# A batched matrix product bound by its transfers: the order of loads and stores in the software queue, from x w s w s to x s s w w

## The chip, the cores and the metric

The kernel runs on one core of a Trainium2 chip. Times are device microseconds of that core. A "span" is the profiled execution alone; it is about 2 us shorter than the time of the run. For each kernel that ran there is one trace, of one of its runs. The experiments ran beside runs of the kernel before on the same chip.

## The reference, cut

```
batch, m, k, n = 32, 512, 1024, 768          # float32
def reference(x, weight):
    return np.matmul(x, weight).astype(np.float32)
```

Per batch: 2.10 MB of x, 3.15 MB of weights in, 1.57 MB out. In all 167.8 MB read and 50.3 MB written.

## The kernel before

Weights and x are cast to bf16 on their way in; they go through the software queue that GpSimd (POOL) issues, and so do most stores. x comes for two batches at once. PE transposes x with an identity matrix, multiplies, and VectorE and ScalarE copy the sums to the output tile. The parts that matter:

```python
    AHEAD = 3
    LATE = 4
    HELD = 3
    # ... (cut)
    w_pool = ctx.enter_context(tc.tile_pool(name="w", bufs=4))
    x_pool = ctx.enter_context(tc.tile_pool(name="x", bufs=3))
    out_pool = ctx.enter_context(tc.tile_pool(name="out", bufs=7))
    # ... (cut)
        for b in range(B):
            if b % 2 and b + AHEAD + 1 < B:
                if b + AHEAD + 1 == B - 1:
                    load_last()
                else:
                    load_pair(b + AHEAD + 1)
            if b + AHEAD < B:
                load_w(b + AHEAD)
            if b <= B - LATE:
                if b > 0:
                    pending.append(b - 1)
                if b + AHEAD < B - HELD or b == B - LATE:
                    for at in pending:
                        nc.gpsimd.dma_start(out=out_view[at], in_=outs[at])
                    pending = []
            # ... (the last stores go to the SyncE queue; transposes, matmuls, copies)
```

With x for a pair of batches, w for the weights of one batch and s for a store of one batch, the queue repeats x w s w s. The last seven stores are held back until all loads are issued.

## Time and profile before

| | before |
|---|---|
| median of the first 3 runs | 517.4 us (517.32 to 517.96) |
| profiled run, its span | 515.96 us, 514.2 us |
| PE busy | 85% |
| the two DMA queues, share of 16 engines | 96.5% + 4.1% |
| HBM traffic over the span | 424 GB/s |

Read the strip of 40 slices first: the transfers are the resource that is never free. Then the waits: past the start, PE idles for weights (28.8 us in all) and for little else (10.2 us in short waits for VectorE). The lines are in the prediction below. One more view of the page of the kernel before: the chain that ended last, as shares of the span, and the table of issues with their time to landing (KB each, then us).

```profile
PE 61%; DMA 25%; DVE 6%; another core or an unknown queue 4%; issue 1%; SPq 1%; ACT 0%
...
w_sb<-in_weight_dram POOLq DMA_DIRECT2D x28, 1536.0 KB, 45.5
out_dram<-out_sb POOLq DMA_DIRECT2D x28, 1536.0 KB, 45.8
```

The chain spends 61% in PE although PE is not the bound: in a loop where a weight's load waits for PE to free a buffer and PE waits for a load issued 45 us ago, the path may run through either. The 45 us from issue to landing are the depth of the queue.

### The profile page before, as it was taken

How to read it: one execution, taken by the hardware profiler on the slowest of the kernel's cores; microseconds unless marked ns; L12 is line 12 of the kernel's file. 1: busy time of each engine (PE TensorE's matmuls, PEld its weight loads, DVE VectorE, ACT ScalarE, POOL GpSimd, SP SyncE). 2: the span in 40 equal slices, each digit the busy share in tenths (PEclk: the TensorE clock that was granted, in tenths of full speed). 3: DMA queues.
4: the chain of work that ended last, by engine and by line, in shares of the span. 5: the costliest groups of instructions: out<-in, count | busy, mean ns of one | idle time of the engine just before them, and what ended most of it. 6: DMA issues, size and time to landing. Idle time of an engine off the chain costs nothing.

```text
span 514.2 us, 5846 instructions
## 1 busy us (share of the span) xinstructions
PE 438.1 (85%) x2576; PEld 279.6 (54%) x2576; DVE 130.0 (25%) x196; ACT 76.1 (15%) x129; POOL 43.8 (9%) x87
## 2 busy tenths in 40 slices
PE   2808999999999797998979889798897979999992
PEld 1506566666666463664636546365564645666561
DVE  1205142323223141231413205032050510514121
ACT  0100111111121111111111111011111111110211
POOL 3000100101010100101001000100001001011000
PEclk9957999999999898898989989799898997999997
DMA  8999999999999999999999999999999999999997
GB/s 240 224 220 214 221 265 289 214 278 273 272 287 213 282 270 276 279 215 293 263 277 275 221 292 250 278 278 224 305 239 277 277 235 306 224 276 214 270 428 318
DMA packets 12904, 135.63 MB, mean 264 GB/s; under 512 B 1488, under 2 KB 1488, under 8 KB 3280
## 3 DMA queue, kind: packets, MB, share of 16 engines
q0 software_dynamic: 11664, 126.88, 96.5%
q1 hardware_dynamic: 1216, 8.39, 4.1%
q8 instruction: 20, 0.33, 0.2%
q14 instruction: 4, 0.03, 0.0%
HBM read 167.77 MB, written 50.33 MB: 424 GB/s over the span
## 4 chain that ended last, share of the span: by engine, by line
PE 61%; DMA 25%; DVE 6%; another core or an unknown queue 4%; issue 1%; SPq 1%; ACT 0%
PE pm L121 54%; DMA w_sb<-in_weight_dram 18%; DMA out_sb<-in_x_dram 7%; PE pt L76 6%; DVE xT L83 4%; DVE out_sb L133 2%; SPq L143 1%; PE pt L103 0%; DVE xT L91 0%; ACT out_sb L134 0%; SPq L140 0%
## 5 line engine op out<-in xcount | busy, mean ns | idle before, releaser
L121 PE MATMUL pm<-w_sb,xT 128*128 128x256 bf16 (+1 forms) x2048 | 356.5, 338 | 28.8 <-DMA w_sb<-in_weight_dram 28.8
L121 PEld LDWEIGHTS <-xT 128*128 128x128 bf16 x2048 | 206.3, 101 | 174.6 <-DMA w_sb<-in_weight_dram 32.1
L133 DVE COPY out_sb<-pm 128x512 f32<-128x512 f32 x64 | 44.2, 691 | 331.8 <-PE pm L121 314.5
L76 PE MATMUL pt<-ident,x_sb 128*128 128x128 f32 x496 | 79.8, 302 | 10.5 <-DVE xT L83 10.2
L76 PEld LDWEIGHTS pt<-ident,x_sb 128*128 128x128 f32 x496 | 69.2, 209 | 21.5 <-DVE xT L83 18.7
L83 DVE COPY xT<-pt 128x1024 bf16<-128x1024 bf16 x120 | 77.4, 687 | 11.0 <-PE pt L76 11.0
L132 ACT COPY out_sb<-pm 128x512 f32<-128x512 f32 x64 | 37.4, 585 | 283.6 <-PE pm L121 276.0
L134 ACT COPY out_sb<-pm 128x512 f32<-128x512 f32 x64 | 37.5, 585 | 144.1 <-PE pm L121 144.0
L68 POOL DMA_DIRECT2D w_sb<-in_weight_dram x37 | 19.7, 533 | 328.7 <-PE pm L121 298.9
L167 POOL DMA_DIRECT2D out_dram<-out_sb x28 | 15.0, 536 | 60.3 <-DMA w_sb<-in_weight_dram 22.7
L103 PE MATMUL pt<-ident,out_sb 128*128 128x128 f32 x8 | 1.9, 421 | 16.2 <-DMA out_sb<-in_x_dram 16.2
L103 PE MATMUL pt<-ident,x_sb 128*128 128x128 f32 x24 | 5.2, 377 | 10.4 <-DMA x_sb<-in_x_dram 10.3
L104 DVE CAST xT<-pt 128x512 bf16<-128x512 f32 x8 | 5.9, 734 | 31.4 <-PE pt L103 31.1
L58 POOL DMA_DIRECT2D x_sb<-in_x_dram x15 | 8.0, 533 | 33.4 <-DMA out_dram<-out_sb 22.6
L103 PEld LDWEIGHTS pt<-ident,out_sb 128*128 128x128 f32 x8 | 1.6, 218 | 16.5 <-issue 16.5
L103 PEld LDWEIGHTS pt<-ident,x_sb 128*128 128x128 f32 x24 | 4.1, 210 | 11.3 <-issue 10.2
L91 DVE COPY xT<-pt 128x1024 bf16<-128x1024 bf16 x4 | 2.6, 686 | 0.2 <-PE pt L76 0.2
L132 ACT ACT_TABLE_LOAD x1 | 1.3, 1283 | 0.7 <-PEq L221 0.7
L62 POOL DMA_DIRECT2D x_sb<-in_x_dram x1 | 0.5, 527 | 6.7 <-DMA w_sb<-in_weight_dram 6.7
masks.py:199 POOL TENSOR_SCALAR_AFFINE_SELECT ident<-ident 128x128 f32<-128x128 f32 x1 | 0.3, 287 | 0.1
masks.py:197 POOL MEMSET ident<- 128x128 f32 x1 | 0.2, 223 | 0.0
L221 POOL MEMSET const-float32-0.0<- 128x1 f32 x1 | 0.1, 98 | 0.2 <-issue 0.2
(3 smaller groups left out, 0.3 us busy)
## 6 DMA issues: line engine op xcount, KB each, us to landing
w_sb<-in_weight_dram POOLq DMA_DIRECT2D x28, 1536.0 KB, 45.5
out_dram<-out_sb POOLq DMA_DIRECT2D x28, 1536.0 KB, 45.8
x_sb<-in_x_dram POOLq DMA_DIRECT2D x15, 2048.0 KB, 52.1
w_sb<-in_weight_dram POOLq DMA_DIRECT2D x7, 768.0 KB, 38.3
out_dram<-out_sb SPq DMA_DIRECT2D x4, 768.0 KB
out_dram<-out_sb SPq DMA_DIRECT2D x2, 1536.0 KB
x_sb<-in_x_dram SPq DMA_DIRECT2D x1, 1536.0 KB
x_sb<-in_x_dram POOLq DMA_DIRECT2D x1, 1024.0 KB, 36.2
```

The source lines that it names most:

```text
L58: nc.gpsimd.dma_start(out=xs[b], in_=pair_view[b // 2])
L68: nc.gpsimd.dma_start(out=ws[b][:, at:at + n, :], in_=w_view[b, :, at:at + n, :])
L76: nc.tensor.transpose(pt[:, j, :], pairs[:, mo, j::JT], ident)
L83: nc.vector.tensor_copy(both[:, :, :, :, half, :].rearrange("p b j i r -> p j b i r"), words(b, mt + MT * half).rearrange("p j (b i r) -> ...
L103: nc.tensor.transpose(pt[:, i, :], rows[:, JT * h + i::KT], ident)
L104: nc.vector.tensor_copy(xT[:, 2 * h:2 * h + 2].rearrange("p j m r -> p j r m"), pt.rearrange("p (j r) m -> p j r m", r=2),)
L121: nc.tensor.matmul(pm[bank][:, at:at + size], xT[:, ko // 2, :, ko % 2], ws[b][:, ko, off:off + size], start=(ko == 0 and not (together an ...
L132: nc.scalar.copy(o[:, 0:512], pm[0])
L133: nc.vector.tensor_copy(o[:, 512:1024], pm[1])
L134: nc.scalar.copy(o[:, 1024:N2], pm[2])
L143: nc.sync.dma_start(x_fourth[rows, 0], x_view[0, rows, MT - 1])
L167: nc.gpsimd.dma_start(out=out_view[at], in_=outs[at])
```

## The change

Its intent: let loads and stores alternate less, and let no weight be followed by a store. Two stores follow each pair of x, two weights follow the stores.

```diff
+            if 0 < b <= B - LATE:
+                pending.append(b - 1)
+            if b % 2 and b + AHEAD < B - HELD:
+                flush()
             if b + AHEAD < B:
                 load_w(b + AHEAD)
-            if b <= B - LATE:
-                if b > 0:
-                    pending.append(b - 1)
-                if b + AHEAD < B - HELD or b == B - LATE:
-                    for at in pending:
-                        nc.gpsimd.dma_start(out=out_view[at], in_=outs[at])
-                    pending = []
+            if b == B - LATE:
+                flush()
```

`flush()` issues the stores in `pending` and empties it. Sizes, counts, buffers and all other engines' work stay.

More of the change, by code (lines that the diff above doesn't have):

```diff
@@ L153, with flush @@
         pending = []
+        def flush():
+            while pending:
+                at = pending.pop(0)
+                nc.gpsimd.dma_start(out=out_view[at], in_=outs[at])
         for b in range(B):
```

## The prediction

> **What bounds the kernel now.** I read the profile page from the top, then the chain of waits, then the timeline of one pair of batches, then the landings of the single transfers. The first view is the strip of 40 slices with the queues below it.
>
> ```profile
> PE   2808999999999797998979889798897979999992
> ...
> DMA  8999999999999999999999999999999999999997
> ...
> q0 software_dynamic: 11664, 126.88, 96.5%
> q1 hardware_dynamic: 1216, 8.39, 4.1%
> ...
> HBM read 167.77 MB, written 50.33 MB: 424 GB/s over the span
> ```
>
> The reader is to see that the DMA row is at 9 from the second slice to the second last, while PE shows 7s and 8s in the second half. The two queues together fill 100.6% of the 16 engines' span (above 100% because packets overlap a little). 218.1 MB in 514.2 us is 424 GB/s: the kernel is bound by its transfers, and the engines never stand without one.
>
> Second, the list of waits (who waited for whom, us in total, times, the longest):
>
> ```profile
> PE pm L121 <- DMA w_sb<-in_weight_dram: 28.8, 10, 3.8
> ...
> POOL out_dram L167 <- DMA w_sb<-in_weight_dram: 22.7, 8, 3.4
> ```
>
> and the timeline (start and length in us, then what, and in brackets PE's idle time before it) at the start of two even batches:
>
> ```profile
> 265.86 12.25 PE L121 MATMUL pm<-w_sb,xT 128*128 128x512 bf16 x64 [3.27 <-DMA w_sb<-in_weight_dram]
> ...
> 424.83 13.19 PE L121 MATMUL pm<-w_sb,xT 128*128 128x512 bf16 x64 [3.75 <-DMA w_sb<-in_weight_dram]
> ```
>
> PE waits for weights ten times, about 3 us each. From 170 us on it does so once per pair of batches, always before the even batch. It lives at the pace of the transfers, one pair every 31.8 us: the weights of batch 12 landed at 202.39 and those of batch 26 at 424.78, 222.39 us for seven pairs. A pair moves 6.29 MB of weights, 4.19 MB of x and 3.15 MB of output, 13.63 MB, so 429 GB/s in this stage. PE has some 28.5 us of work in it (10.4 us for the odd batch, about 12.4 us for the even one, which starts at half clock after its wait, and 5.7 us of transposes between).
>
> The software queue is never short. The median time from issue to landing is 45.5 us for a whole weight. The built program reuses eight completion semaphores in turn, so from 150 us on an issue also waits for the transfer eight places ahead; that is what "POOL out_dram waits for w_sb" is. At such a wait seven transfers are still queued. POOL's remaining waits are for PE (298.9 us) and starve nothing.
>
> **What the Trainium skill says.** "DMA: Bandwidth & Descriptors", section Bandwidth, gives 425 GB/s for a 16 MB load on one core and 435 GB/s as the ceiling of the ports; here the span has 424 and the steady stage 429, so the trace agrees, and little is left to win in this resource. The same page, section Queues, rings and completion order, says that each engine takes the rings in turn, packet by packet, and starts one ring's descriptors in ring order; the landings agree, since the whole transfers of the software queue land in the order of their issue. "TensorE: Matmul & The Clock Gate", Part 1, has a PE at half clock after an idle window of about 3.4 us; here the even batch after its wait takes 12 to 13.4 us against 10.4. No page gives a cost for a turn from loading to storing, which is what the change is about.
>
> **The change, part by part.** The order of issue per pair (x, s for a store, w for a weight) goes from x w s w s to x s s w w. Counts, sizes, buffers and the work of PE, VectorE and ScalarE stay.
>
> *Turns removed.* A period of before goes w to s, s to w, w to s, s to x: four turns. After, it has x to s and s to w: two. There are 28 stores on the software queue, the last three already in a row; so about 26 groups of stores become about 14 and some 24 turns go. Their price I read from the distance between landings in the steady stage. A store takes 3.65 to 3.69 us, an x pair 9.65, a weight behind a store 7.24 to 7.47 (mean 7.37 of eight), a weight behind an x 7.27 to 7.47 (mean 7.33). Early, where nothing but loads is in the queue, a weight takes 7.29, an x pair 9.67. So a turn costs at most 0.04 to 0.08 us per transfer. A second reading: most weight packets take 926 ns; those cut across by a store are stretched, up to 1.6 us, and all such excess over the run adds up to 1.3 us per engine. Weights lose it, x packets ahead of stores may inherit some. Saving: 24 x 0.04, about 1 us, 0.5 to 1.3 us of transfer time.
>
> *The even weight moves back.* In a steady period the odd weight has the same transfers ahead of it as before. The store of batch b-1, which stood behind the even weight w(b+3), now stands ahead of it; so the even weight lands one store, 3.7 us, later. The x pair has one store fewer ahead and lands 3.7 us earlier, which nobody needs. PE waits before just those even batches. But this is a shift, not a cost per pair: once PE is 3.7 us later in phase, it releases everything 3.7 us later, its period is still that of the transfers, and each wait is again 31.8 minus 28.5, about 3.3 us. PE's total wait for weights should rise once by about 3.7 us, to 32 or 33 us. The odd weight then has room: it lands about 7.4 us after the even one, and PE needs 18 us to get there.
>
> *Does it starve the queue?* Issues of weights come 3.7 us later against the stream. Their lead is 45 us and would be 41. No.
>
> *The end.* After the wait at 424.8 us PE works without a wait for weights to its last matmul near 504; so the shift of 3.7 us, less about 1 us of saved transfer time, reaches the end of PE's chain, some 3 us later. Now the transfers there. The last two half stores of the last batch are issued at 503.3 and 504.6 and land at 511.2 and 513.1, 1.84 us apart, each behind a backlog: 7.9 and 8.5 us instead of perhaps 3.9 for one on a free queue (estimate: 1.84 us of data and 2 us of latency). Issued 3 us later they would want to land at 510.2 and 512.0 or later because of one another: inside the old times. The slack of about 1 us swallows the shift, and the gain in transfer time is capped by PE's chain. **Sum:** minus 1.0 us for turns, plus 0 to 1 us at the end: 517.4 becomes about 517.2 us.
>
> **The rivals.** (1) *Turns are dearer than the landings show*, because two directions in flight together share something all the time. For it: the second half runs at 429 GB/s in the steady stage and the early loads alone near 431 (3.146 MB of weight in 7.29 us). Against: even if every byte ran at 431, the span would shrink by 0.5%, 2.5 us; that would give about 515. (2) *The shift of the even weight becomes the bound at the end*: the whole 3.7 us reaches PE's last matmul, the longer idle time costs another half-clock window (up to 1.7 us of lost work), and the last stores then find an empty queue. For it: PE runs without slack from 424.8 to 504. Against: the backlog of stores at that point. It would give 519 to 521. (3) *POOL's order blocks*: a store now stands ahead of the even weight and must wait for the copies of batch b-1. Those copies end about 0.3 us after the matmuls that the weight waits for anyway, so the issue slips by under 1 us in a lead of 45. It would change nothing. (4) *All is hidden*: same time to a few tenths. That is near my own sum.
>
> **Range and chances.** Centre 517.2. Rival 1 reaches down to 515, rival 2 up to about 520 or 521; I give each one chance in ten of its far half, so 515.5 to 519.5 eight times in ten. Two per cent is 10.3 us, and neither is near it: within 2% 0.97, faster 0.02, slower 0.01.
>
> **What would show it.** Right: DMA at 9 through the strip and 423 to 427 GB/s over the span; weight landings 7.3 us apart; PE's waits for weights still before even batches, about 3.3 us each, total about 32 us; the first such wait larger, or one pair earlier; the last matmul at 506 to 509; the last store with a shorter time from issue to landing. Weight packets over 926 ns nearly gone. Wrong: a period clearly under 31.5 us (turns matter), a wait for weights of 6 us or more in each pair (the phase argument fails), DMA under 9 in a slice before the last (starving), or an end set by PE with the transfers idle behind it.

## The result, and the profile after

| | before | changed |
|---|---|---|
| median, same rounds, 6 runs each | 517.36 us (515.72 to 518.04) | 515.36 us (514.95 to 515.68) |
| profiled run, its span | 515.96, 514.2 us | 514.95, 513.2 us |
| HBM traffic over the span | 424 GB/s | 425 GB/s |
| PE's waits for weights | 28.8 us, 10 times | 32.0 us, 11 times |
| last weight landed | 486.9 us | 486.1 us |
| last store landed | 513.1 us | 512.1 us |

The ratio is 0.9967, with a 95% interval of 0.9948 to 0.9985. It is the mean time of one kernel's runs over that of the other's of the same rounds, so not quite the ratio of the medians. By the 2% rule the two are the same; the small gain is clear of noise.

From the page of the changed kernel: the strip, the queues, the chain, and issues with their time to landing.

```profile
PE   2808999999989697998979979799797997999995
...
DMA  8999999999999999999999999999999999999997
...
q0 software_dynamic: 11664, 126.88, 96.6%
...
HBM read 167.77 MB, written 50.33 MB: 425 GB/s over the span
...
DMA 51%; PE 40%; DVE 5%; issue 1%; SPq 1%; ACT 0%
...
w_sb<-in_weight_dram POOLq DMA_DIRECT2D x28, 1536.0 KB, 41.9
out_dram<-out_sb POOLq DMA_DIRECT2D x28, 1536.0 KB, 42.6
```

The transfers are as full as before. The time to landing of a weight fell by 3.6 us, one store: POOL issues later against the stream, because PE runs later. The chain turned round, from 61% PE to 51% DMA, with 1 us less span: its shares do not measure a gain.

The list of waits, and the timeline of PE at its first waits for weights (start, length, idle time before in brackets):

```profile
PE pm L121 <- DMA w_sb<-in_weight_dram: 32.0, 11, 4.9
```

```profile
142.85 10.58 PE L121 MATMUL pm<-w_sb,xT 128*128 128x512 bf16 x64 [1.67 <-DMA w_sb<-in_weight_dram]
174.41 11.98 PE L121 MATMUL pm<-w_sb,xT 128*128 128x512 bf16 x64 [4.91 <-DMA w_sb<-in_weight_dram]
205.97 13.24 PE L121 MATMUL pm<-w_sb,xT 128*128 128x512 bf16 x64 [3.51 <-DMA w_sb<-in_weight_dram]
...
427.50 13.41 PE L121 MATMUL pm<-w_sb,xT 128*128 128x512 bf16 x64 [3.35 <-DMA w_sb<-in_weight_dram]
```

The same view of the kernel before begins one pair later:

```profile
170.69 12.26 PE L121 MATMUL pm<-w_sb,xT 128*128 128x512 bf16 x64 [2.88 <-DMA w_sb<-in_weight_dram]
```

PE meets the stream one pair earlier (1.67 us of waiting), is put back by the rest of the shift at the next even batch (4.91 against 2.88), and then waits about 3.3 us per pair as before. From these lines the pace of the stream can be read: 427.50 minus 174.41 is 253.09 us for eight pairs, 31.64 per pair; in the kernel before 424.83 minus 170.69 is 254.14, so 31.77.

At the end, the windows of the changed kernel (from and to, length, busy time of PE, PEld, DVE, ACT and POOL, clock, DMA share, GB/s):

```profile
500.00:505.00 5.00, 5.00 (x33) 3.04 (x31) 0.00 (x0) 0.13 (x1) 0.00 (x0) 1.00 1.00 423
505.00:507.00 2.00, 1.85 (x12) 0.88 (x9) 1.02 (x2) 1.70 (x4) 0.00 (x0) 1.00 0.68 283
507.00:509.00 2.00, 0.00 (x0) 0.00 (x0) 0.36 (x1) 0.47 (x1) 0.00 (x0) 1.00 1.02 418
```

and of the kernel before:

```profile
505.00:507.00 2.00, 0.00 (x0) 0.00 (x0) 0.00 (x0) 0.00 (x0) 0.00 (x0) 1.00 0.99 415
```

PE's end moved from 504 to 507 us, and for 2 us a third of the transfer engines have nothing to do. That hole looks like a loss of some 0.6 us (a third of 2 us). An experiment will say whether it is one.

Two readings of the single DMA packets in the traces carry the rest. The *landing of the last weight* is the time at which the same bytes have passed, so it compares streams without the end of the program; I give the mean over the 16 engines, which is steadier than the last of them. The *lengthened packets*: almost every packet of a kind takes the same time (a weight's 926 ns, an x pair's 1227, a store's 460); what single ones take above that, summed and divided by 16, is time lost per engine. (Stores of more than some 600 ns are left out of the sum, because they are hard to tell from short weights. Counting them adds up to 0.1 us, but 0.5 us in the last row of the table below.)

### The profile page after: what moved, and what is told of

The parts are those of the page before. It is cut to its first block, busy times and chain, and to the rows that moved or that the text cites. A ratio compares the mean times of both kernels' runs of the same rounds, so it can differ in the third digit from the quotient of the medians.

```text
span 513.2 us, 5846 instructions
## 1 busy us (share of the span) xinstructions
PE 437.9 (85%) x2576; PEld 279.4 (54%) x2576; DVE 129.9 (25%) x196; ACT 76.3 (15%) x129; POOL 44.1 (9%) x87
## 4 chain that ended last, share of the span: by engine, by line
DMA 51%; PE 40%; DVE 5%; issue 1%; SPq 1%; ACT 0%
DMA w_sb<-in_weight_dram 45%; PE pm L121 35%; DMA out_sb<-in_x_dram 7%; PE pt L76 5%; DVE xT L83 4%; DVE out_sb L133 2%; SPq L143 1%; PE pt L103 0%; DVE xT L91 0%; ACT out_sb L134 0%; SPq L140 0%
## 5 line engine op out<-in xcount | busy, mean ns | idle before, releaser
L76 PE MATMUL pt<-ident,x_sb 128*128 128x128 f32 x496 | 79.8, 302 | 10.4 <-DVE xT L83 10.1
L103 PE MATMUL pt<-ident,x_sb 128*128 128x128 f32 x24 | 5.0, 371 | 10.4 <-DMA x_sb<-in_x_dram 10.2
## 6 DMA issues: line engine op xcount, KB each, us to landing
w_sb<-in_weight_dram POOLq DMA_DIRECT2D x28, 1536.0 KB, 41.9
```

Source lines behind the costliest of these rows:

```text
L76: nc.tensor.transpose(pt[:, j, :], pairs[:, mo, j::JT], ident)
L103: nc.tensor.transpose(pt[:, i, :], rows[:, JT * h + i::KT], ident)
```

## The experiments

The first theory: each turn from loading to storing or back costs a little; halving the turns gives the gain, and the late end of PE gives part of it back. Rivals: only a weight followed by a store costs; the later place of the even weight is what helps; it all happens at the end.

### The changed kernel again

No edit.

> The changed kernel once more, on the same chip as the next three, as their yardstick. First theory (turns less phase): a turn between loading and storing costs about 0.055 us of transfer time, 24 turns fewer save 1.3 to 1.5 us; the later even weight makes PE end late, so that the transfers idle 0.5 us near 506 us and give a third of it back. Expected 515.4 us, 1.0 to 2.0 us below the kernel before. The rival theories expect the same of this run.

Measured: 515.09 us (515.00 to 515.49) against 516.36 of the kernel before; ratio 0.9981 (0.9965 to 0.9996). The kernel before had 11 runs on this chip, from 514.96 to 517.50. So its best run equals the changed kernel's. What differs is how often it is slow, and the size of the gain depends on which of its runs one meets.

### Two turns, but a weight is followed by a store: x w w s s

```diff
+            if b + AHEAD < B:
+                load_w(b + AHEAD)
             if 0 < b <= B - LATE:
                 pending.append(b - 1)
-            if b % 2 and b + AHEAD < B - HELD:
-                flush()
-            if b + AHEAD < B:
-                load_w(b + AHEAD)
-            if b == B - LATE:
+            if (b % 2 == 0 and b + AHEAD < B - HELD) or b == B - LATE:
                 flush()
```

> Order x w w s s: two turns per pair as in the changed kernel, but a weight is followed by a store and the even weight keeps its old place. First theory (any turn costs): the pair period is again 31.66 us as in the changed kernel, PE's last matmul is back near 504 us, no idle transfers at the end; 0.3 to 0.7 us below the changed kernel, about 514.9. Rival (only a weight followed by a store costs, because its packets are stretched): half of the gain is lost, period about 31.71, so 0.2 to 0.5 us above the changed kernel. Rival (the later place of the even weight is what helps): all of the gain is lost, the time of the kernel before.

Measured: 515.26 us (515.08 to 515.47), ratio 0.9982 (0.9968 to 0.9996), the time of the changed kernel. The even weight is back in its old place and PE's last matmul near 503 us, and a weight is followed by a store in every pair. Timeline of PE, first and last of eight pairs:

```profile
170.80 12.03 PE L121 MATMUL pm<-w_sb,xT 128*128 128x512 bf16 x64 [3.19 <-DMA w_sb<-in_weight_dram]
...
423.82 13.50 PE L121 MATMUL pm<-w_sb,xT 128*128 128x512 bf16 x64 [3.26 <-DMA w_sb<-in_weight_dram]
```

253.02 us for eight pairs, 31.63 each. So what the change's words promise, no store behind a weight, is not what is needed, and the place of the even weight gives nothing. The 0.3 to 0.7 us that I expected from the earlier end of PE did not come.

### Four turns with the weights late: x s w s w

```diff
-            if b % 2 and b + AHEAD < B - HELD:
+            if b + AHEAD < B - HELD:
                 flush()
```

> Order x s w s w: four turns per pair as in the kernel before, but the even weight one store later as in the changed kernel, and one weight per pair followed by a store instead of two. First theory: period 31.77 as before, plus the idle 0.5 us at the end, so the kernel before or up to 0.5 us above it. Rival (only a weight followed by a store costs): half of the stream's gain, period about 31.71, some 0.7 us below the kernel before less the 0.5 at the end, so 0 to 0.4 below. Rival (the place of the weight helps): the time of the changed kernel.

Measured: 517.02 us (515.82 to 518.48), ratio 1.0018 (0.9998 to 1.0038): the level of the kernel before or a little above, and its wide spread. One of its weights per pair is followed by a store, not two, yet its traced run (518.2 us) is the slower one. Eight pairs:

```profile
175.16 12.71 PE L121 MATMUL pm<-w_sb,xT 128*128 128x512 bf16 x64 [5.09 <-DMA w_sb<-in_weight_dram]
...
430.08 13.24 PE L121 MATMUL pm<-w_sb,xT 128*128 128x512 bf16 x64 [3.54 <-DMA w_sb<-in_weight_dram]
```

254.92 us, 31.87 per pair. Its x packets, which now stand ahead of a single store, are lengthened by 0.94 us in sum, where those of the kernel before have 0.09. So x is no safer ahead of a store than a weight is; the rival about weights falls.

### The end of PE moved back: the changed kernel with two even weights ahead of their stores

```diff
+            if b in (23, 25):
+                load_w(b + AHEAD)
             if b % 2 and b + AHEAD < B - HELD:
                 flush()
-            if b + AHEAD < B:
+            if b + AHEAD < B and b not in (23, 25):
                 load_w(b + AHEAD)
```

> The changed kernel, except that the even weights of batches 26 and 28 go ahead of the two stores of their pair; the stream is otherwise that of the changed kernel. First theory: the wait before batch 26 falls from 3.35 us to nothing, PE's last matmul comes at 500 to 502 us instead of 507, the hole in the transfers near 506 us is gone, and the time is 0.4 to 0.6 us below the changed kernel. A rival that sees no cost at the end expects the same time as the changed kernel to 0.1 us.

Measured: 515.43 us (515.15 to 515.84), ratio 0.9985 (0.9971 to 1.0000), against 515.09 for the changed kernel of the same rounds. The edit did its part: the wait before batch 26 is gone and the last matmul comes at 501. The hole is gone too, but the windows show where the time went:

```profile
505.00:507.00 2.00, 0.00 (x0) 0.00 (x0) 0.00 (x0) 0.00 (x0) 0.00 (x0) 0.72 0.99 415
507.00:509.00 2.00, 0.00 (x0) 0.00 (x0) 0.00 (x0) 0.00 (x0) 0.00 (x0) 0.50 0.97 406
509.00:511.00 2.00, 0.00 (x0) 0.00 (x0) 0.00 (x0) 0.00 (x0) 0.00 (x0) 0.50 0.71 298
511.00:513.00 2.00, 0.00 (x0) 0.00 (x0) 0.00 (x0) 0.00 (x0) 0.00 (x0) 0.50 0.10 43
```

The engines now run dry one after another from 508.5 to 512, where in the changed kernel they end together, from 511.0 to 511.6. In the changed kernel's hole at least six of the 16 engines were busy at every moment: the fast ones idled, the slowest did not. The landings show it: the store ahead of the last two landed on its last engine at 508.4, and two half stores of 8 packets of 234 ns each, 3.7 us, bring that engine to 512.1, where the last store did land. The slowest engine set this program's end, and the hole cost nothing. My expectation of 0.4 to 0.6 us missed.

### More turns, first series: weights and stores cut in two along their rows' contents

Weights are loaded as two halves of four k-rows each, stores as two halves of columns. The turns per pair are 2, 4 and 8. The core of the edit:

```diff
-        for n in CHUNKED.get(b, (KT,)):
+        for n in CHUNKED.get(b, (KT // 2, KT // 2)):
             nc.gpsimd.dma_start(out=ws[b][:, at:at + n, :], in_=w_view[b, :, at:at + n, :])
             at += n
+            if between:                        # 8 turns only: a half store behind each half weight
+                store_half(*between.pop(0))
```

> Dose series, weights and stores of the middle stage each cut into two transfers: x, four half stores, four half weights, so 2 turns per pair. All theories: near the changed kernel, 515 to 516 us, if the cutting itself costs little; this run and the next fix that cost.

> Dose series, same cuts, order of the kernel before: x, two half weights, two half stores, twice: 4 turns per pair, 2 of them weight to store. First theory (each turn costs on average, some of them a stall of 0.2 to 0.5 us): 1 to 2 us above the run with 2 turns, and a wider spread from run to run. A rival that gives the gain to the place of the weights or to the end of the program: no order in this series, all within 0.5 us.

> Dose series, same cuts, half weight and half store in turn: 8 turns per pair, 4 of them weight to store. First theory: 2 to 5 us above the run with 4 turns, landing of the last weight later by as much, spread wider still. If a turn costs only where a transfer runs long enough for the engines to drift apart, no more than the run with 4 turns. If the place of the weights is what counts: the time of the run with 4 turns to 0.3 us, since the even weight has half a store more ahead of it.

Measured: 517.90 (517.61 to 518.20), 517.77 (517.41 to 518.92) and 517.58 us (517.45 to 517.64). The last weight landed at 489.05, 489.04 and 489.06 us on the slowest engine; as a mean of the engines, the measure used elsewhere, at 487.51, 487.81 and 487.12. Turns cost nothing here in the time, and by either measure eight cost no more than two: the first theory as I had put it, a price per turn, falls. (The rival that expected no order in this series had its reason in the place of the weights or the end of the program, and those two had fallen in the runs above.) The cut itself costs some 2 us: while only loads are under way (40 to 60 us) the packets move 430.9 GB/s against 432.2.

The lengthened packets gave a hint why. A half weight's packets take 473 ns; of some 8070, 53, 130 and 51 took more than 490. So lengthening is nearly absent with 2 turns and with 8, and more frequent in the one in the middle, which also has the wider spread and the latest mean landing.

### Fewer turns: stores in groups of four

```diff
-            if b % 2 and b + AHEAD < B - HELD:
+            if b % 4 == 1 and b + AHEAD < B - HELD:
                 flush()
```

This version keeps the seven output buffers.

> Whole transfers again, stores in groups of four behind every second x pair: 1 turn per pair on average. First theory: 0.2 to 0.7 us below the changed kernel in the landing of the last weight; the time itself may be the same, because the slowest engine and PE's end set it, or worse by some us if an output buffer is not stored in time for the batch seven later. A rival that gives the gain only to weights that are not followed by a store expects no gain at all over the changed kernel, since there are none left.

Measured: 516.06 us (515.54 to 516.64), ratio 0.9989 (0.9968 to 1.0010); five of its six runs lie above 515.55 and two of the changed kernel's twelve do. The last weight landed at 485.04 us (mean of the engines) against 484.97 there: fewer turns than one group of stores per pair bring nothing. Here the end may cost something. Windows:

```profile
505.00:507.00 2.00, 2.00 (x15) 1.22 (x13) 0.00 (x0) 0.35 (x1) 0.00 (x0) 1.00 0.78 326
507.00:509.00 2.00, 1.63 (x11) 0.73 (x8) 1.24 (x2) 1.70 (x4) 0.00 (x0) 1.00 0.24 98
```

PE ends 2 us later still, for 0.15 us (508.67 to 508.82) no transfer engine at all was busy, and the time is 0.7 to 1.0 us above the two medians of the changed kernel (of other rounds, and one of them on another chip). By the same sum as above, 509.2 plus 3.7 us, the last store would have landed at 512.9 without the hole; it landed at 513.2. So some 0.3 us are the end's, and the rest is not explained. This is the rival that the prediction feared, in a kernel that goes further, and here its cost is small.

### The kernel before again

> The kernel before as a run of its own, for a second trace and six more times. If the lengthened packets at the turns carry the loss, their sum in this trace should go with its time: 0.8 to 1.0 us per engine where the run takes 515.0 us, 1.7 at 516.0, near 2.5 at 518. Spread 514.9 to 518.0, ratio 1.00. A rival that sees a fixed cost per turn expects the same sum of lengthened packets as in the first trace, 1.7 us, whatever the time.

Measured: 515.85 us (515.10 to 517.64), ratio 0.9994 (0.9971 to 1.0018). Its traced run took 515.48 us and has 1.39 us of lengthened packets, between the 0.84 of the changed kernel and the 1.71 of the first trace (515.96 us). The price is not fixed per turn; it goes with the time of the run. The pairs say it more directly:

```profile
234.01 12.23 PE L121 MATMUL pm<-w_sb,xT 128*128 128x512 bf16 x63 [2.83 <-DMA w_sb<-in_weight_dram]
265.55 13.51 PE L121 MATMUL pm<-w_sb,xT 128*128 128x512 bf16 x63 [3.24 <-DMA w_sb<-in_weight_dram]
```

This pair, with its four turns, took 31.54 us, and five of the eight pairs from 170.89 to 424.81 us took 31.54 to 31.58: as little as a pair of the changed kernel. The loss sits in single pairs (the last took 32.44). One of them is no order's doing: the pair that ends near 360 us takes about 0.5 us more than its neighbours in the changed kernel too (332.18 to 364.38, 32.20 us), and 32.0 to 32.3 us in every other version with whole transfers and stores in ones or twos.

### More turns, second series: cut by partitions, so that packets keep their size

Weights and stores as two transfers of 64 partitions each, with 2 turns per pair and with 8.

```diff
+        if b not in CHUNKED:
+            for rows in (slice(0, P // 2), slice(P // 2, P)):
+                nc.gpsimd.dma_start(out=ws[b][rows], in_=w_view[b, rows])
+                if between:                    # 8 turns only
+                    store_half(*between.pop(0))
+            return
```

> Second dose series, weights and stores cut by partitions, so that the packets keep the size they have in the kernel before and only their number per transfer halves: x, four half stores, four half weights, 2 turns per pair. Expected near the changed kernel, 515 to 516 us, with a narrow spread; it is the control of the next run.

> Same cut by partitions, half weight and half store in turn: 8 turns per pair with packets of full size. If the first dose series (517.9, 517.8, 517.6 us for 2, 4, 8 turns) showed no cost because its packets were half as large, this run is 1 to 4 us slower than its control, with more lengthened packets and a wide spread. If the number of turns never matters, it is within 0.3 us of its control, and what the change does must lie in something else that it alters, such as a single store between two loads.

Measured: 529.50 (528.27 to 532.32) and 527.03 us (525.31 to 530.35). As times these are inconclusive: the cut spoiled the early stage of pure loading (375 GB/s at 40 to 60 us in both, against 432), and the control was not near the changed kernel. In the later stage the run with 8 turns took 32.24 us per pair (183.60 to 441.48 over eight) and its control 31.85 (185.73 to 440.54). So the run with eight turns was made once more with its first four weights whole:

```diff
+        if b < 4:
+            nc.gpsimd.dma_start(out=ws[b], in_=w_view[b])
+            return
```

> The 8-turn order with packets of full size once more, but the first four weights whole, because the cut by partitions spoiled the stage of pure loading at the start (375 GB/s between 40 and 60 us against 432) and so hid the answer in the time. In the steady stage the 8-turn run took 32.24 us per pair and its 2-turn control 31.85, the control mostly 31.6. If turns between whole packets cost, this run keeps about 32.2 us per pair, 0.45 us above the kernel before over some 12 pairs, so 518 to 522 us, and its load packets that overlap a store are lengthened by 2 us per engine or more. If the number of turns does not matter, its pair takes 31.75 us and the run 516 to 517.

Measured: 519.34 us (518.83 to 521.50) against 516.10 for the kernel before; ratio 1.0072 (1.0049 to 1.0095). This run, with packets of full size and eight turns, is slower by 3 us. But not evenly. Timeline of PE at its waits:

```profile
143.85 10.56 PE L137 MATMUL pm<-w_sb,xT 128*128 128x512 bf16 x64 [2.69 <-DMA w_sb<-in_weight_dram]
176.18 12.71 PE L137 MATMUL pm<-w_sb,xT 128*128 128x512 bf16 x64 [5.70 <-DMA w_sb<-in_weight_dram]
208.30 12.02 PE L137 MATMUL pm<-w_sb,xT 128*128 128x512 bf16 x64 [3.35 <-DMA w_sb<-in_weight_dram]
...
398.78 12.24 PE L137 MATMUL pm<-w_sb,xT 128*128 128x512 bf16 x64 [3.26 <-DMA w_sb<-in_weight_dram]
430.36 11.93 PE L137 MATMUL pm<-w_sb,xT 128*128 128x512 bf16 x64 [3.28 <-DMA w_sb<-in_weight_dram]
```

The first two pairs take 32.3 and 32.1 us, the last one 31.58, which is what a pair takes in the changed kernel when nothing disturbs it (31.54 to 31.57). The same order is dear early and free late. The 32.2 us in every pair that I expected were not there. This run has no control of its own with 2 turns, so how much of the 3 us is the cut's is not shown. It may be much: the control with 2 turns and all weights cut also lost early and not late (pairs of 33.30 and 32.87 us up to 186 us, then 31.80, 31.60 and 31.60). Its lengthened packets sum to about 11 us per engine, over half of it in x packets, and of some 370 lengthened load packets between 60 and 440 us only a third lie at a store, no more than of all load packets there. So packets are also lengthened without a turn beside them.

### What the traces say together

| run (trace) | order | lengthened packets, us per engine | last weight landed, mean of engines, us |
|---|---|---|---|
| stores in fours | x s s s s w w x w w | 0.82 | 485.04 |
| changed, again | x s s w w | 0.83 | 485.02 |
| changed | x s s w w | 0.84 | 484.97 |
| stores last | x w w s s | 0.92 | 485.06 |
| end moved back | x s s w w | 0.97 | 485.15 |
| before, again | x w s w s | 1.39 | 485.23 |
| before | x w s w s | 1.71 | 485.63 |
| single stores first | x s w s w | 2.68 | 486.84 |
| 8 turns, late cut | w and s in halves by turns | 3.76 | 488.70 |

(The stores-last run has one store fewer ahead of that point; 3.67 us, one store's distance between landings, are added.) From the changed kernel to the kernel before the lengthened packets grow by 0.87 us and the landing by 0.66; to the single stores by 1.84 and 1.87. The two go together, as they must where the engines never pause; the sums say where the time sits, and not why. And the lengthened load packets do lie at the turns: between 60 and 440 us, 105 of 117 in the kernel before overlap a store's packet or lie within 0.6 us of one, 151 of 160 with single stores, where of all load packets only 42% and 44% do; in the changed kernel only 39 are lengthened at all, 28 of them so (of all, 20%).

## Why the prediction was right or wrong

**The bound, and starvation: right.** DMA stays at 9 through the strip, traffic is 425 GB/s. The lead of the weights was to fall from 45 to 41 us; it fell to 41.9.

**The even weight as a one-time shift: right.** PE's waits rose from 28.8 to 32.0 us (predicted 32 or 33), one pair earlier and one larger wait, then 3.3 us per pair again.

**Turns: the direction was right, the term mis-sized in kind.** The step "a turn costs at most 0.04 to 0.08 us per transfer", summed as "Saving: 24 x 0.04, about 1 us", treats a turn as having a price. For the pair of traces it held, by luck of the runs that were traced: 0.8 us at the last weight's landing, 1.0 us at the last store's. But the halves series had 2, 4 and 8 turns at one time, and the kernel before moves from 514.9 to 518.1 us over its 56 runs with the same number of turns. What the runs show in its place is an irregular loss, carried by lengthened load packets beside stores: against the changed kernel nothing in the best runs (514.91 and 514.95 us), about 3 us in the worst. The changed kernel (12 runs), the stores-last order (6) and the version with the end moved back (6) never took more than 515.84 us; of the 56 runs of the kernel before, 40 did. The change takes the slow runs away and leaves the fast ones where they are: the mean of 56 is 516.45, that of the changed kernel's 12 is 515.25, so the average gain is 1.2 us. The 2.0 us between the medians of the first rounds were a good draw.

**The second reading, "x packets ahead of stores may inherit some": right.** The weights' excess fell from 1.26 to 0.21 us, that of x rose from 0.09 to 0.33.

**The end: right in its steps, wrong in one conclusion.** PE ended near 507 (predicted 506 to 509), and the last two stores needed 4.0 and 4.6 us from issue to landing instead of 7.9 and 8.5; they landed at 510.2 and 512.1, forecast were 510.2 and 512.0. (The forecast 3.9 us on a free queue had no trace behind the part that is not data.) But "the gain in transfer time is capped by PE's chain" failed: with PE's end moved back by 6 us the kernel was no faster. The slowest transfer engine ends the program, and it still had a backlog. So the term of "0 to 1 us at the end" was 0. The sum as written gives 516.4 to 517.4, and my centre, near its upper end, forecast a gain of 0.2 us where the average one is 1.2. The rest of the miss is the base: 517.4 was the median of three runs and lies 1 us above the mean of 56. The measured 515.36 lies just below the range given eight chances in ten (515.5 to 519.5).

**The rivals.** Dearer turns (down to 515) came nearest to the measured time, by the irregular loss rather than by a share of all bytes. The shift as a bound at the end was not met by the change, and by the stores in fours with some 0.3 us. Its "up to 1.7 us of lost work" in a half-clock window was low: the even batches that the prediction shows took 12.25 and 13.19 us against 10.4. The hidden-anyway rival was wrong by those 1 to 2 us.

**What stays open.** Why a load packet is lengthened beside a store in one pass and not in the next; why the runs cut by partitions lose early and not late; why halves of 12 KB per packet read hardly do it. The traces name no engine for a packet. How far the engines drift apart can still be read from the 16 landings of each transfer: between 60 and 440 us the first and the last are on average 2.7 us apart in the kernel before, 2.8 in the changed one and 3.0 with single stores, so drift does not sort these orders. No version here beat the changed kernel: the stores-last order matches it.

## What to carry to other kernels

Where transfers are the bound, try stores in groups in the queue rather than one by one between loads: here one group of two per pair was enough, and groups of four gave nothing more and pushed PE's end past the transfers' backlog. Read a gain below half a per cent from many runs of both kernels, since it may lie in the spread and not in the best time. And before spending effort on a hole in the DMA strip near the end, ask whether the slowest engine has it too.

## What the Trainium skill lacked or had wrong

- "DMA: Bandwidth & Descriptors" has no word on loads and stores by turns in one queue: here 31.54 to 31.57 us per pair undisturbed, and on average 31.62 to 31.64 with paired stores (three traces), 31.74 and 31.77 in the kernel before and 31.87 with single stores first.
- The same page, section Rules for kernel authors, asks for 128 partitions and at least 1 MiB per DMA, which the runs bear out for the partitions. No page has a rate for the two halves of a tile queued one after the other and cast from float32 to bf16 on the way: weights of 1.5 MB read per transfer on 64 partitions fell to 375 GB/s where whole ones had 432; the same bytes on 128 partitions with rows half as long kept 430.9.
- The same page, section Latency and other measured facts, calls engines 7 and 15 usually slower, without an amount. The traces name no engine, but in the kernel before the last store's first and last engine landed 3.1 us apart (509.9 and 513.1), in the changed one, after the hole, 0.9 us (511.2 and 512.1).
